# Row gather, cumulative sum and projection: groups of 512 rows instead of whole batches, one cast and one store per group

## The chip, the cores and the metric

The kernel runs on one core of one Trainium2 chip; the other cores are idle. A time is the device time of one execution in microseconds (us). The median of three timed executions is given; a profile is taken in an execution of its own, with every instruction and every DMA packet recorded. Engine names in the profile: PE is TensorE (PEld its weight loads), DVE is VectorE, ACT is ScalarE, POOL is GpSimd, SP is SyncE, which here only issues DMAs.

## The reference

```python
def setup_inputs():
    B, S, N, D = (16, 4096, 2048, 512)
    # x: float32 (B, S, D); indices: int64 (B, N), sorted, distinct; w: float32 (D, D)

def reference(x, indices, w):
    gathered = x[b_idx, indices, :]        # (B, N, D): 2048 of 4096 rows of each batch
    cs = np.cumsum(gathered, axis=1)       # along the 2048 gathered rows
    return np.matmul(cs, w)                # (B, N, D) float32
```

For each of 16 batches, 2048 rows of 512 floats (2 KB each) are fetched by index, summed up cumulatively along the rows, and each sum is multiplied by a 512 x 512 matrix. 67 MB are read and 67 MB written.

## The kernel before

A tile is 128 rows; a batch has NT = 16 tiles, the whole problem 256. The columns are cut into DC = 4 chunks of 128.

- **Indices.** `load_indices(b)` loads one batch's 2048 indices (16 KB, SP's queue), takes the low words as floats on VectorE (L62), transposes them on TensorE (L64) and writes them back as integers, one column per tile (L66). It runs four batches ahead. The weights w (1 MB) are loaded first, on the same queue, and cast to fp16 by VectorE (L51, L52).
- **Gather and cast.** For each tile GpSimd issues an indirect DMA that fetches 128 rows into `g32[:, t, :]` (L79), and ScalarE casts them to fp16 into `g16` (L86). `g32` holds a whole batch (16 tiles, fp32), with two buffers: the first gather of batch b waits until all 16 casts of batch b-2 are done.
- **Cumulative sum.** For each tile four matmuls take the gathered rows as stationary operand and an upper triangle of ones `ut` as moving operand (L93): the result `pa` (PSUM, two buffers) is the sum within the tile, transposed, 128 columns of d by 128 rows for each of four chunks. VectorE adds the last column of the tile before (the carry) and writes fp16 into `csT` (L106; the first tile of a batch is only copied, L103). `csT` too holds a whole batch and has two buffers.
- **Projection.** For each tile four matmuls of 512 columns take `csT` as stationary operand and w as moving operand (L116) and accumulate in `pb` (PSUM, five buffers). Even tiles are copied to `ob` by VectorE (L125), odd ones by ScalarE (L127); then SP stores the 256 KB (L128). `ob` has twelve buffers. Each partition holds one row, so a store is 128 runs of 2 KB.

The program is written out without loops. The framework puts the instructions of each engine in order by a priority, which is the order of writing unless `high_priority` moves it (L101), and by its own estimate of when each is ready; each engine then works in that order. All semaphores are placed by the framework. In the order of writing, a batch's 16 tiles of gathers and casts come first, then 16 of cumulative sums, then 16 of projections.

Of the kernel before, what the change touches and what calls it, by code (L numbers as in the profile page):

```python
# [1 line left out]

# [5 lines left out]

P = 128  # L10
FP32 = mybir.dt.float32
FP16 = mybir.dt.float16
U32 = mybir.dt.uint32


@with_exitstack
def kernel(
    ctx: ExitStack,
    tc: tile.TileContext,
    x: bass.AP,  # L20
    indices: bass.AP,
    w: bass.AP,
    out: bass.AP,
):
    nc = tc.nc

    B, S, D = x.shape
    N = indices.shape[1]
    assert D == 512 and N % P == 0

    NT = N // P
    DC = D // P
    PREF = 3

    x_flat = x.rearrange("b s d -> (b s) d")
    idx_u32 = indices.bitcast(U32)

    const = ctx.enter_context(tc.tile_pool(name="const", bufs=1))
    idxp = ctx.enter_context(tc.tile_pool(name="idxp", bufs=6))
    gp = ctx.enter_context(tc.tile_pool(name="gp", bufs=2))  # L40
    big = ctx.enter_context(tc.tile_pool(name="big", bufs=2))
    outp = ctx.enter_context(tc.tile_pool(name="outp", bufs=12))
    psA = ctx.enter_context(tc.tile_pool(name="psA", bufs=2, space=bass.MemoryType.PSUM))
    psB = ctx.enter_context(tc.tile_pool(name="psB", bufs=5, space=bass.MemoryType.PSUM))

    ut = const.tile([P, P], FP16)
    make_upper_triangular(nc, ut[:], 1.0, diag=True)

    w16 = const.tile([P, DC, D], FP16)
    w32 = const.tile([P, DC, D], FP32)  # L50
    nc.sync.dma_start(out=w32[:], in_=w.rearrange("(c p) d -> p c d", p=P))  # L51
    nc.vector.tensor_copy(out=w16[:], in_=w32[:])  # L52

    id16 = const.tile([16, 16], FP32)
    make_identity(nc, id16[:])
    idxgs = {}

    def load_indices(b):
        idx64 = idxp.tile([16, P], mybir.dt.int64, name="idx64")
        nc.sync.dma_start(out=idx64[:], in_=indices[b].rearrange("(t p) -> t p", p=P))  # L60
        idxf = idxp.tile([16, P], FP32, name="idxf")
        nc.vector.tensor_copy(out=idxf[:], in_=idx64[:].bitcast(U32)[:, 0::2])  # L62
        idx_ps = psB.tile([P, 16], FP32, name="idx_ps", tag="pb")
        nc.tensor.transpose(out=idx_ps[:], in_=idxf[:], identity=id16[:])  # L64
        idxg = idxp.tile([P, NT], U32, name="idxg")
        nc.vector.tensor_copy(out=idxg[:], in_=idx_ps[:])  # L66
        idxgs[b] = idxg

    for bb in range(4):
        load_indices(bb)  # L70

    for b in range(B):
        if b + 4 < B:
            load_indices(b + 4)
        idxg = idxgs.pop(b)
        g32 = gp.tile([P, NT, D], FP32, name="g32")
        g16 = big.tile([P, NT, D], FP16, name="g16")
        for t in range(NT):
            nc.gpsimd.indirect_dma_start(  # L79
                out=g32[:, t, :],  # L80
                out_offset=None,
                in_=x_flat,
                in_offset=bass.IndirectOffsetOnAxis(ap=idxg[:, t : t + 1], axis=0),
                element_offset=b * S * D,
            )
            nc.scalar.copy(out=g16[:, t, :], in_=g32[:, t, :])  # L86

        csT = big.tile([P, DC, N], FP16, name="csT")

        for t in range(NT):  # L90
            pa = psA.tile([P, DC * P], FP32, name="pa")
            for c in range(DC):
                nc.tensor.matmul(  # L93
                    out=pa[:, c * P : (c + 1) * P],
                    lhsT=g16[:, t, c * P : (c + 1) * P],
                    rhs=ut[:],
                    start=(c == 0),
                    stop=(c == DC - 1),
                )
            pa3 = pa[:].rearrange("p (c n) -> p c n", c=DC)  # L100
            with tc.high_priority(offset=200):  # L101
                if t == 0:
                    nc.vector.tensor_copy(out=csT[:, :, 0:P], in_=pa3)  # L103
                else:
                    carry = csT[:, :, t * P - 1 : t * P].broadcast_to([P, DC, P])
                    nc.vector.tensor_tensor(  # L106
                        out=csT[:, :, t * P : (t + 1) * P],
                        in0=pa3,
                        in1=carry,
                        op=mybir.AluOpType.add,  # L110
                    )

        for t in range(NT):
            pb = psB.tile([P, D], FP32, name="pb")
            for c in range(DC):
                nc.tensor.matmul(  # L116
                    out=pb[:],
                    lhsT=csT[:, c, t * P : (t + 1) * P],
                    rhs=w16[:, c, :],
                    start=(c == 0),  # L120
                    stop=(c == DC - 1),
                )
            ob = outp.tile([P, D], FP32, name="ob")
            if t % 2 == 0:
                nc.vector.tensor_copy(out=ob[:], in_=pb[:])  # L125
            else:
                nc.scalar.copy(out=ob[:], in_=pb[:])  # L127
            nc.sync.dma_start(out=out[b, t * P : (t + 1) * P, :], in_=ob[:])  # L128


# [1 line left out]
_INS = ['x', 'indices', 'w']  # L132
_OUTS = [((16, 2048, 512), 'float32')]


# [23 lines left out]
```

## Time and profile before

| | |
|---|---|
| timed executions | 381.35, 381.68, 379.84 us; median 381.35 |
| profiled execution, first to last instruction | 595.4 us; no time of its own beside the span was recorded |
| mean TensorE clock granted in it | 0.776 |
| DMA | 135.96 MB in 58416 packets, 228 GB/s over the span |
| GpSimd gathers (L79) | 256, 949 ns each |
| TensorE projection, cumulative sum (L116, L93) | 1024 of 434 ns, 1024 of 238 ns |
| VectorE carry add (L106), copy (L125) | 240 of 689 ns, 128 of 688 ns |
| ScalarE cast (L86), copy (L127) | 256 of 620 ns, 128 of 586 ns |

The groups of the page read: line, engine, operation, output<-input, shape, count | busy us in all, mean ns of one | idle time of the engine just before them, and who ended it. In the list of waits a row is: who waited <- for whom: us in all, times, longest. In the DMA view a queue's row is: packets, MB, and the time its packets took as a share of 16 DMA engines over the window. q0 is the queue of the gathers, q1 that of SP's loads and stores. The profiled execution is much longer than the timed ones, so a sum made from its rows has to be held against both.

### The profile page before, as it was taken

The numbers are of one execution on the slowest core, as the hardware profiler recorded it, in microseconds if no ns is written. First come the engines' busy times: TensorE is split into PE (matmuls) and PEld (weight loads), VectorE is DVE, ScalarE is ACT, GpSimd is POOL, SyncE is SP. The second block draws the span as 40 slices with busy tenths as digits, with TensorE's granted clock in tenths as the row PEclk, the third lists the DMA queues.
The fourth block names the chain that finished last, engine by engine and source line by source line (L and its number), as shares of the span: only waits on it lengthen the run. The fifth ranks groups of instructions, "written<-read, shape, count | busy, mean of one in ns | idle before, by whom it ended". The sixth has DMA issues, their size and how long they took to land.

```text
span 595.4 us, 6309 instructions
## 1 busy us (share of the span) xinstructions
PE 359.3 (60%) x2064; PEld 177.9 (30%) x2064; DVE 260.1 (44%) x417; ACT 208.7 (35%) x385; POOL 243.7 (41%) x264
## 2 busy tenths in 40 slices
PE   0413653746464791829558284582855838559997
PEld 0201231323232341414224142241422414225553
DVE  2202352425253572516327163361642717339885
ACT  1302353333160453307034070350703507045722
POOL 3772737372717254450714507236072360710000
PEclk9855967566969895868759677596785968869999
DMA  4774969584859678674857748568385684855565
GB/s 141 215 223 143 296 220 295 165 314 162 284 192 307 222 268 293 225 220 177 290 179 243 243 164 288 183 231 263 149 295 187 216 279 189 290 197 211 214 233 227
DMA packets 58416, 135.96 MB, mean 228 GB/s; under 512 B 8464, under 2 KB 8720, under 8 KB 58384
## 3 DMA queue, kind: packets, MB, share of 16 engines
q0 software_dynamic: 20480, 67.13, 37.2%
q1 hardware_dynamic: 37904, 68.44, 30.7%
q8 instruction: 16, 0.26, 0.2%
q14 instruction: 16, 0.13, 0.1%
HBM read 68.42 MB, written 67.11 MB: 228 GB/s over the span
## 4 chain that ended last, share of the span: by engine, by line
PE 49%; another core or an unknown queue 32%; issue 8%; DVE 7%; DMA 2%; POOL 1%; ACT 1%; DVEq 0%; ACTq 0%
PE pb L116 38%; PE pa L93 11%; DVE csT L106 3%; DVE csT L103 2%; DVE ob L125 2%; DMA w<-in_w_dram 1%; POOL g L79 1%; DMA g<-in_x_dram,idxg 1%; ACT ob L127 0%; ACT g L86 0%; DVE w L52 0%; PE idx_ps L64 0%; DVE idxf L62 0%; DVE idxg L66 0%
## 5 line engine op out<-in xcount | busy, mean ns | idle before, releaser
L79 POOL DMA_INDIRECT g<-in_x_dram,idxg x256 | 242.8, 949 | 280.0 <-ACT g L86 198.7
L116 PE MATMUL pb<-w,csT 128*128 128x512 f16 x1024 | 307.6, 434 | 18.9 <-DVE ob L125 13.1
L106 DVE TENSOR_TENSOR csT<-pa,csT 128x512 f16<-128x512 f32 x240 | 165.3, 689 | 148.9 <-remote 91.0
L93 PE MATMUL pa<-ut,g 128*128 128x128 f16 x1024 | 109.0, 238 | 196.1 <-DVE csT L106 91.9
L127 ACT COPY ob<-pb 128x512 f32<-128x512 f32 x128 | 75.1, 586 | 352.6 <-remote 163.8
L93 PEld LDWEIGHTS <-g 128*128 128x128 f16 x1024 | 81.7, 106 | 278.5 <-issue 188.1
L125 DVE COPY ob<-pb 128x512 f32<-128x512 f32 x128 | 87.7, 688 | 164.1 <-remote 87.9
L86 ACT CAST g<-g 128x512 f16<-128x512 f32 x256 | 141.8, 620 | 29.9 <-DMA g<-in_x_dram,idxg 16.5
L116 PEld LDWEIGHTS <-csT 128*128 128x128 f16 x1024 | 103.3, 110 | 111.6 <-issue 61.3
L64 PE MATMUL idx_ps<-id,idxf 16*128 16x16 f32 x16 | 3.4, 252 | 17.1 <-DVE idxf L62 8.3
L103 DVE CAST csT<-pa 128x512 f16<-128x512 f32 x16 | 11.0, 690 | 6.0 <-remote 2.6
L64 PEld LDWEIGHTS idx_ps<-id,idxf 16*128 16x128 f32 x16 | 2.3, 158 | 22.8 <-issue 11.4
L62 DVE CAST idxf<-idx 16x128 f32<-16x128 uint32 x16 | 3.2, 215 | 2.6 <-DMA idx<-in_indices_dram 2.4
L52 DVE CAST w<-w 128x2048 f16<-128x2048 f32 x1 | 1.2, 1227 | 6.8 <-DMA w<-in_w_dram 6.8
L66 DVE CAST idxg<-idx_ps 128x16 uint32<-128x16 f32 x16 | 2.5, 171 | 2.8 <-PE idx_ps L64 2.4
L86 ACT ACT_TABLE_LOAD x1 | 1.3, 1283 | 0.7 <-PEq L143 0.7
masks.py:65 POOL MEMSET ut<- 128x128 f16 x1 | 0.2, 205 | 0.3 <-POOLq L143 0.3
masks.py:66 POOL TENSOR_SCALAR_AFFINE_SELECT ut<-ut 128x128 f16<-128x128 f16 x1 | 0.3, 284 | 0.0
L143 POOL MEMSET const-float32-0.0<- 128x1 f32 x1 | 0.1, 104 | 0.2 <-issue 0.2
masks.py:199 POOL TENSOR_SCALAR_AFFINE_SELECT id<-id 16x16 f32<-16x16 f32 x1 | 0.2, 190 | 0.0
L143 POOL MEMSET const-uint8-127<- 128x1 uint8 x1 | 0.1, 124 | 0.0
L143 POOL MEMSET const-bfloat16-1.0<- 128x1 bf16 x1 | 0.1, 118 | 0.0
(2 smaller groups left out, 0.2 us busy)
## 6 DMA issues: line engine op xcount, KB each, us to landing
out_dram<-ob SPq DMA_DIRECT2D x256, 256.0 KB
g<-in_x_dram,idxg POOLq DMA_INDIRECT x256
w<-in_w_dram SPq DMA_DIRECT2D x1, 1024.0 KB
idx<-in_indices_dram SPq DMA_DIRECT2D x16, 16.0 KB
```

The lines of the kernel that those rows point to most:

```text
L52: nc.vector.tensor_copy(out=w16[:], in_=w32[:])
L62: nc.vector.tensor_copy(out=idxf[:], in_=idx64[:].bitcast(U32)[:, 0::2])
L64: nc.tensor.transpose(out=idx_ps[:], in_=idxf[:], identity=id16[:])
L66: nc.vector.tensor_copy(out=idxg[:], in_=idx_ps[:])
L79: nc.gpsimd.indirect_dma_start(out=g32[:, t, :], out_offset=None, in_=x_flat, in_offset=bass.IndirectOffsetOnAxis(ap=idxg[:, t : t + 1], a ...
L86: nc.scalar.copy(out=g16[:, t, :], in_=g32[:, t, :])
L93: nc.tensor.matmul(out=pa[:, c * P : (c + 1) * P], lhsT=g16[:, t, c * P : (c + 1) * P], rhs=ut[:], start=(c == 0), stop=(c == DC - 1),)
L103: nc.vector.tensor_copy(out=csT[:, :, 0:P], in_=pa3)
L106: nc.vector.tensor_tensor(out=csT[:, :, t * P : (t + 1) * P], in0=pa3, in1=carry, op=mybir.AluOpType.add,)
L116: nc.tensor.matmul(out=pb[:], lhsT=csT[:, c, t * P : (t + 1) * P], rhs=w16[:, c, :], start=(c == 0), stop=(c == DC - 1),)
L125: nc.vector.tensor_copy(out=ob[:], in_=pb[:])
L127: nc.scalar.copy(out=ob[:], in_=pb[:])
```

## The change

The batch as unit is given up. The 256 tiles form 64 groups of R = 4 tiles (512 rows, four groups to a batch), and one loop runs over the groups: the cumulative sum of group g, tile by tile, alternates with the projection of group g-1.

- All indices come in two loads of 128 KB at the start, on SP, and are transposed 128 x 128; w is loaded on ScalarE's queue and cast by ScalarE.
- Gathers have the same form, one per tile, and are written nine groups ahead (`AHEAD`); `g32` holds a group and has nine buffers.
- One ScalarE instruction casts a group's four tiles; `g16` and `csT` hold a group and have four buffers each, `pa` has three.
- The triangle `ut` is reordered, so that row n of a tile goes to column n // 4 of quarter n % 4 of `csT`: after four tiles, the stationary operand j holds the rows 4p + j of the group. The result of projection j then has row 4p + j in partition p, and the four results side by side in `ob` make 8 KB of one partition that are also 8 KB in a row in the output.
- Of a group's four results VectorE copies the first, ScalarE three; one store of 1 MB per group, 128 runs of 8 KB. `ob` holds a group and has five buffers.

```diff
+    R = 4
+    Q = P // R
+    T = B * NT
+    G = T // R
+    GB = NT // R
+    AHEAD = 9
...
-    idxp = ctx.enter_context(tc.tile_pool(name="idxp", bufs=6))
-    gp = ctx.enter_context(tc.tile_pool(name="gp", bufs=2))
-    big = ctx.enter_context(tc.tile_pool(name="big", bufs=2))
-    outp = ctx.enter_context(tc.tile_pool(name="outp", bufs=12))
-    psA = ctx.enter_context(tc.tile_pool(name="psA", bufs=2, space=bass.MemoryType.PSUM))
+    gp = ctx.enter_context(tc.tile_pool(name="gp", bufs=AHEAD))
+    g16p = ctx.enter_context(tc.tile_pool(name="g16p", bufs=4))
+    csp = ctx.enter_context(tc.tile_pool(name="csp", bufs=4))
+    outp = ctx.enter_context(tc.tile_pool(name="outp", bufs=5))
+    psA = ctx.enter_context(tc.tile_pool(name="psA", bufs=3, space=bass.MemoryType.PSUM))
...
+    for k in range(KI):                      # KI = 2
+        nc.sync.dma_start(out=idx64[:, k, :], in_=idx_rows[k * P : (k + 1) * P, :])
+    nc.scalar.dma_start(out=w32[:], in_=w.rearrange("(c p) d -> p c d", p=P))
+    make_identity(nc, ident[:])              # 128 x 128
+    ut = const.tile([P, R, Q], FP16)
+    nc.gpsimd.memset(ut[:], 1.0)
+    nc.gpsimd.affine_select(out=ut[:], in_=ut[:], compare_op=mybir.AluOpType.is_ge, fill=0.0,
+        base=0, pattern=[[1, R], [R, Q]], channel_multiplier=-1)
+    for k in range(KI):
+        nc.vector.tensor_copy(out=idxf[:, k, :], in_=idx64[:, k, :].bitcast(U32)[:, 0::2])
+        nc.tensor.transpose(out=idx_ps[:], in_=idxf[:, k, :], identity=ident[:])
+        nc.vector.tensor_copy(out=idxg[:, k, :], in_=idx_ps[:])
+    nc.scalar.copy(out=w16[:], in_=w32[:])
...
+    def gather(g):
+        g32 = gp.tile([P, R, D], FP32, name="g32")
+        for r in range(R):
+            t = g * R + r
+            nc.gpsimd.indirect_dma_start(out=g32[:, r, :], ...)
+
+    def cumsum_tile(g, r):
+        if r == 0:
+            cst[g] = csp.tile([P, DC, R, P], FP16, name="csT")
+            g16s[g] = g16p.tile([P, R, D], FP16, name="g16")
+            nc.scalar.copy(out=g16s[g][:], in_=gs.pop(g)[:])
+        pa = psA.tile([P, DC, R, Q], FP32, name="pa")
+        for c in range(DC):
+            nc.tensor.matmul(out=pa[:, c], lhsT=g16[:, c * P : (c + 1) * P], rhs=ut[:], ...)
+        dst = csT[:, :, :, r * Q : (r + 1) * Q]
+        ...                                  # first tile of a batch: tensor_copy(dst, pa)
+        nc.vector.tensor_tensor(out=dst, in0=pa[:],
+            in1=last.unsqueeze(2).broadcast_to([P, DC, R, Q]), op=mybir.AluOpType.add)
+
+    def project_tile(g, r):
+        pb = psB.tile([P, D], FP32, name="pb")
+        for c in range(DC):
+            nc.tensor.matmul(out=pb[:], lhsT=csT[:, c, r, :], rhs=w16[:, c, :], ...)
+        if r == 0:
+            nc.vector.tensor_copy(out=obs[g][:, r, :], in_=pb[:])
+        else:
+            nc.scalar.copy(out=obs[g][:, r, :], in_=pb[:])
+        if r == R - 1:
+            b, h = divmod(g, GB)
+            dst = out[b, h * R * P : (h + 1) * R * P, :].rearrange("(p j) d -> p j d", j=R)
+            nc.sync.dma_start(out=dst, in_=obs.pop(g)[:])
+
+    for g in range(AHEAD):
+        gather(g)
+    for g in range(G + 1):
+        if g + AHEAD < G:
+            gather(g + AHEAD)
+        for r in range(R):
+            if g < G:
+                cumsum_tile(g, r)
+            if g > 0:
+                project_tile(g - 1, r)
```

The `high_priority` block around the carry add is gone, and so is the per-batch `load_indices`.

More of the change, by code (lines that the diff above doesn't have):

```diff
@@ L6 @@
 from concourse import bass_utils, mybir
-from concourse.masks import make_upper_triangular, make_identity
+from concourse.masks import make_identity
 from concourse._compat import with_exitstack
@@ L41 @@
-    big = ctx.enter_context(tc.tile_pool(name="big", bufs=2))
-    outp = ctx.enter_context(tc.tile_pool(name="outp", bufs=12))
-    psA = ctx.enter_context(tc.tile_pool(name="psA", bufs=2, space=bass.MemoryType.PSUM))
-    psB = ctx.enter_context(tc.tile_pool(name="psB", bufs=5, space=bass.MemoryType.PSUM))
-    ut = const.tile([P, P], FP16)
-    make_upper_triangular(nc, ut[:], 1.0, diag=True)
-    w16 = const.tile([P, DC, D], FP16)
-    w32 = const.tile([P, DC, D], FP32)
-    nc.sync.dma_start(out=w32[:], in_=w.rearrange("(c p) d -> p c d", p=P))
@@ L52 @@
[L52 to L78, printed above, removed]
+    gp = ctx.enter_context(tc.tile_pool(name="gp", bufs=AHEAD))
+    g16p = ctx.enter_context(tc.tile_pool(name="g16p", bufs=4))
+    csp = ctx.enter_context(tc.tile_pool(name="csp", bufs=4))
+    outp = ctx.enter_context(tc.tile_pool(name="outp", bufs=5))
@@ new lines @@
+    ident = const.tile([P, P], FP32)
+    make_identity(nc, ident[:])
+    ut = const.tile([P, R, Q], FP16)
+    nc.gpsimd.memset(ut[:], 1.0)
+    nc.gpsimd.affine_select(
+        out=ut[:],
+        in_=ut[:],
+        compare_op=mybir.AluOpType.is_ge,
+        fill=0.0,
+        base=0,
+        pattern=[[1, R], [R, Q]],
+        channel_multiplier=-1,
+    )
+    idxf = const.tile([P, KI, P], FP32)
+    idxg = const.tile([P, KI, P], U32)
+    for k in range(KI):
+        nc.vector.tensor_copy(out=idxf[:, k, :], in_=idx64[:, k, :].bitcast(U32)[:, 0::2])
+        idx_ps = psB.tile([P, P], FP32, name="idx_ps", tag="pb")
+        nc.tensor.transpose(out=idx_ps[:], in_=idxf[:, k, :], identity=ident[:])
+        nc.vector.tensor_copy(out=idxg[:, k, :], in_=idx_ps[:])
@@ L79 @@
+    w16 = const.tile([P, DC, D], FP16)
+    nc.scalar.copy(out=w16[:], in_=w32[:])
+    gs = {}
+    cst = {}
+    g16s = {}
+    def gather(g):
+        g32 = gp.tile([P, R, D], FP32, name="g32")
+        gs[g] = g32
+        for r in range(R):
+            t = g * R + r
             nc.gpsimd.indirect_dma_start(
-                out=g32[:, t, :],
+                out=g32[:, r, :],
                 out_offset=None,
                 in_=x_flat,
-                in_offset=bass.IndirectOffsetOnAxis(ap=idxg[:, t : t + 1], axis=0),
@@ L84 @@
-                element_offset=b * S * D,
-            )
[L86 to L128, printed above, removed]
+                in_offset=bass.IndirectOffsetOnAxis(ap=idxg[:, t // P, t % P : t % P + 1], axis=0),
@@ new lines, in gather @@
+                element_offset=(t // NT) * S * D,
+            )
+    def cumsum_tile(g, r):
[3 more added lines that the diff above has]
+            nc.scalar.copy(out=g16s[g][:], in_=gs.pop(g)[:])
+        csT = cst[g]
+        g16 = g16s[g][:, r]
+        pa = psA.tile([P, DC, R, Q], FP32, name="pa")
+        for c in range(DC):
+            nc.tensor.matmul(
+                out=pa[:, c],
+                lhsT=g16[:, c * P : (c + 1) * P],
+                rhs=ut[:],
+                start=(c == 0),
+                stop=(c == DC - 1),
+            )
+        dst = csT[:, :, :, r * Q : (r + 1) * Q]
+        if g % GB == 0 and r == 0:
+            nc.vector.tensor_copy(out=dst, in_=pa[:])
+            return
+        if r == 0:
+            last = cst[g - 1][:, :, R - 1, P - 1 : P]
+        else:
+            last = csT[:, :, R - 1, r * Q - 1 : r * Q]
+        nc.vector.tensor_tensor(
+            out=dst,
+            in0=pa[:],
+            in1=last.unsqueeze(2).broadcast_to([P, DC, R, Q]),
+            op=mybir.AluOpType.add,
+        )
@@ new lines @@
+    obs = {}
+    def project_tile(g, r):
+        if r == 0:
+            obs[g] = outp.tile([P, R, D], FP32, name="ob")
+        csT = cst[g]
+        pb = psB.tile([P, D], FP32, name="pb")
+        for c in range(DC):
+            nc.tensor.matmul(
+                out=pb[:],
+                lhsT=csT[:, c, r, :],
+                rhs=w16[:, c, :],
+                start=(c == 0),
+                stop=(c == DC - 1),
+            )
+        if r == 0:
+            nc.vector.tensor_copy(out=obs[g][:, r, :], in_=pb[:])
+        else:
+            nc.scalar.copy(out=obs[g][:, r, :], in_=pb[:])
[3 more added lines that the diff above has]
+            nc.sync.dma_start(out=dst, in_=obs.pop(g)[:])
```

13 lines of the change are left out of this document (9 added, 4 removed).

## The prediction

> **What bounds the kernel now.** I read the page first (engines, queues, chain, groups), then the waits, then the timeline of the start and of the end, then the DMA queues in single windows.
>
> ```profile
> span 595.4 us, 6309 instructions
> PE 359.3 (60%) x2064; PEld 177.9 (30%) x2064; DVE 260.1 (44%) x417; ACT 208.7 (35%) x385; POOL 243.7 (41%) x264
> ...
> DMA packets 58416, 135.96 MB, mean 228 GB/s; under 512 B 8464, under 2 KB 8720, under 8 KB 58384
> ...
> PE 49%; another core or an unknown queue 32%; issue 8%; DVE 7%; DMA 2%; POOL 1%; ACT 1%; DVEq 0%; ACTq 0%
> ...
> L79 POOL DMA_INDIRECT g<-in_x_dram,idxg x256 | 242.8, 949 | 280.0 <-ACT g L86 198.7
> L116 PE MATMUL pb<-w,csT 128*128 128x512 f16 x1024 | 307.6, 434 | 18.9 <-DVE ob L125 13.1
> L106 DVE TENSOR_TENSOR csT<-pa,csT 128x512 f16<-128x512 f32 x240 | 165.3, 689 | 148.9 <-remote 91.0
> L93 PE MATMUL pa<-ut,g 128*128 128x128 f16 x1024 | 109.0, 238 | 196.1 <-DVE csT L106 91.9
> L127 ACT COPY ob<-pb 128x512 f32<-128x512 f32 x128 | 75.1, 586 | 352.6 <-remote 163.8
> ...
> L125 DVE COPY ob<-pb 128x512 f32<-128x512 f32 x128 | 87.7, 688 | 164.1 <-remote 87.9
> L86 ACT CAST g<-g 128x512 f16<-128x512 f32 x256 | 141.8, 620 | 29.9 <-DMA g<-in_x_dram,idxg 16.5
> ```
>
> The profiled execution is not the timed one: 595.4 us against a median of 381.35. No engine is over 60% busy, and 32% of the chain (191 us) is time whose releaser the trace does not know. So I look for what 381 us can hold, and that starts with GpSimd.
>
> ```profile
> POOL g L79 <- ACT g L86: 198.7, 14, 18.1
> ...
> POOL g L79 <- issue: 73.1, 239, 0.6
> ```
>
> ```profile
> L79 POOL DMA_INDIRECT g<-in_x_dram,idxg x256: 943/949/1102, 9.0 to 523.4; - x128
> ```
>
> ```profile
> L128 SPq DMA_DIRECT2D out_dram<-ob x256: 332/332/1004, 28.3 to 592.0; - x128
> ```
>
> The four rows are two of the list of waits, one of the gather's line, one of the store's. The gathers' train runs from 9.0 to 523.4 us: 242.8 busy, 73.1 of the 0.30 us gap between two gathers, 198.7 in 14 waits for ScalarE's casts to free one of the two 16-tile g32 buffers. The pitch is (242.8+73.1)/256 = 1.234 us, and 1.25 within a batch. From the last gather to the end are 72 us. Without the 14 waits the profiled execution would be 595.4-198.7 = 396.7. The timed 381.35 leave, after a head of 9.0 and a train of 315.9, 56.4 us for the tail and all waits of GpSimd together. So in timed runs the train hardly waits, and the time is head + train + tail. What the tail is, the end of the trace shows, where no gather disturbs:
>
> ```profile
> 554.20:572.90 18.70, 18.14 (x132) 9.77 (x130) 15.67 (x25) 9.08 (x18) 0.00 (x0) 1.00 0.62 235
> ```
>
> One batch of 16 tiles there takes 18.70 us (columns: length, then busy time of TensorE, weight loads, VectorE, ScalarE, GpSimd, granted clock, DMA share, GB/s): TensorE is busy 18.14 at full clock, 1.17 us a tile. When the last gather is issued, up to two batches are still to be projected, because a batch's cumsum of 16 tiles stands ahead of its projection: 2 x 18.7 = 37.4 us, and some of the 56.4 are then waits.
>
> The DMA engines are the second candidate.
>
> ```profile
> DMA packets 1177, 3.04 MB, mean 380 GB/s; under 512 B 188, under 2 KB 188, under 8 KB 1177
> ...
> q0 software_dynamic: 621, 2.03, 69.5%
> q1 hardware_dynamic: 556, 1.01, 32.8%
> ```
>
> ```profile
> q1 hardware_dynamic: 5904, 10.75, 60.1%
> ```
>
> The first fence is the DMA view of 221 to 229 us, the stretch with both queues fullest; the second that of 545 to 592, stores alone. Stores: 10.75 MB in 0.601 x 47 = 28.2 us, 381 GB/s while busy, 0.69 us for 256 KB. Gathers beside stores: 2.03 MB in 0.695 x 8 = 5.56 us, 365 GB/s, 0.72 us. Both at once moved 380 GB/s: 0.524 MB a tile, 1.38 us. That is more than the gather's pitch of 1.25, so the two limits lie within 10% of each other. The timed runs bound it too: (381.35-9.0-37.4)/256 = 1.31 us a tile with a two-batch tail, 1.38 with a one-batch tail.
>
> **The change part by part.**
>
> *Start.* Before, 1 MB of w is loaded ahead of the indices, and w's cast stands ahead of the first index cast:
>
> ```profile
> 0.75 5.99 DMA w<-in_w_dram
> 6.76 1.23 DVE w L52
> 9.03 1.10 POOL g L79
> 15.47 2.99 DMA g<-in_x_dram,idxg
> ```
>
> ```profile
> 7.90 0.75 DVE L62 CAST idxf<-idx 16x128 f32<-16x128 uint32 x5
> ```
>
> ```profile
> masks.py:65 POOL MEMSET ut<- 128x128 f16 x1 | 0.2, 205 | 0.3 <-POOLq L143 0.3
> masks.py:66 POOL TENSOR_SCALAR_AFFINE_SELECT ut<-ut 128x128 f16<-128x128 f16 x1 | 0.3, 284 | 0.0
> ```
>
> These are pieces of the chain of waits, one row of the timeline and two groups of the page. After, the indices come as two 128 KB loads first on SP, w on ScalarE's queue beside them. If they share the rings evenly they land as w did, near 6.0, if not near 2.5; with the 1.13 us from the index cast to the first gather (7.90 to 9.03 before) the train starts between 3.6 and 7.1. I take 5.5, a gain of 3.5. The larger masks on GpSimd, two fills and selects of 128 x 128, take 2 x (0.2+0.3) = 1 us and end before the indices land, even at 2.5; without that cover they would cost the 1 us. w's cast moves to ScalarE, which has no group to cast before 5.5 + 4 x 1.25 + 3 = 13.5 us. Sixteen small index casts, transposes and copies inside the loop become two ahead of it; none was on the path.
>
> *Gathers.* 256 of the same form, same pitch: floor 256 x 1.25 = 320. Their buffer is freed by a group's cast instead of the whole batch's 16: 36 tiles ahead (45 us of train) instead of two lumps of 16. The 198.7 us of waits go; late next is the landing of packets. The new wait, of gather g+9 for cast g, holds up only later gathers.
>
> *Casts.* ScalarE casts 2048 columns at once.
>
> ```profile
> 314.10 2.18 ACT L86 CAST g<-g 128x512 f16<-128x512 f32 x4
> 6.76 1.23 DVE L52 CAST w<-w 128x2048 f16<-128x2048 f32 x1 [6.76 <-DMA w<-in_w_dram]
> ```
>
> Four back to back take 2.18 us, which bounds the new one from above; VectorE's 1.23 for the same shape bounds it from below. I take 2.1, nearer to its own engine: 64 x 2.1 = 134 instead of 141.8.
>
> *Cumsum.* The same matmuls (1024 of 128 columns) and the same 256 VectorE instructions of 128 x 512. Their writes now go in runs of 32 columns instead of 128. No row shows that; I take 689 ns as before. Twice that is the other end: VectorE would need 1.55 us a tile and decide (below).
>
> *Projection and copies.* The same 1024 matmuls. VectorE keeps 64 copies, ScalarE gets 192: VectorE 176+44 = 220 us, ScalarE 134+192 x 0.586 = 247 us. Both stay under the train's 320 and cost nothing beside it; without that cover ScalarE would have 247 to give. TensorE at 1.17 us a tile needs 299 us, also under it, if its clock stays up.
>
> *Stores.* 64 of 1 MB in place of 256 of 256 KB: same bytes, SP has 192 issues of 0.33 us less, off the path. 8 KB runs mean a quarter of the 32,768 store packets. No row has such packets. The ends for 256 KB: a small loss, down to the gathers' 365 GB/s (0.72 us), or a gain at which gather and store fit into GpSimd's pitch (1.25-0.72 = 0.53), beyond which nothing more is won. Nothing in the rows moves faster than 381 GB/s while busy, so I take a small gain, 0.65, and 1.38 becomes 1.34. A store now waits for four copies instead of one; behind it on SP stand only later stores, and an ob buffer is wanted again five groups (26 us) later.
>
> *Train.* Pace between 1.25 (GpSimd) and 1.34 (rings full); 1.29, the middle: 256 x 1.29 = 330.
>
> *Tail.* The last group alone: landing 3.0 (row above), cast 2.1, cumsum of 4 tiles beside the projection of the group before 4 x 1.17 = 4.7, projection 4 x 4 x 0.216 = 3.5, last copy 0.6, then the 1 MB store. A 256 KB store ended 3.4 us after its issue (592.0 to 595.4), 0.69 of it transfer: 2.7 + 1 MB at 380 GB/s, 2.8 = 5.5.
>
> ```profile
> 586.57 4.76 PE pb L116 x22
> ```
>
> This row gives the 0.216 (4.76/22). Sum of the tail 19.4, against at least 37.
>
> *Sum.* 5.5 + 330 + 19.4 = 355 us. Against the timed median that is -26 (head -3.5, tail -18 or more, pace the rest), against the profiled 595.4 it says nothing, since its idle is not in the timed runs.
>
> **The rivals.**
>
> *GpSimd alone decides.* If the rings keep up: 5.5 + 320 + 19.4 = 345, or a little less. For it: gathers never stretch, 943 to 1102 ns.
>
> *The bytes decide.* 135.96 MB in 381.35 us are 356 GB/s already. If that is what the memory gives two mixed streams, the change moves the same bytes and only the head goes: 378. Against it: the 380 GB/s above, over 8 us only; for it:
>
> ```profile
> 248.00:252.00 4.00, 3.09 (x4) 1.00 1.01 322
> ```
>
> In this stretch in the middle of the trace (length, GpSimd's busy time, granted clock, DMA share, GB/s) rings that are full move 322 GB/s.
> The Trainium skill's page "DMA: Bandwidth & Descriptors", section "Where 436 GB/s comes from", says that for transfers between HBM and SBUF a core's share of about 358 GB/s binds; by it 136 MB need 380 us, and nothing would be gained. The trace's 380 GB/s speaks against it for a core alone on the chip.
>
> *The cast is exposed (slower).* ScalarE works in order. If the cast of group g+1 stands behind the last copy of group g-1, TensorE can't start the cumsum of g+1 until it is done: 4.7 of TensorE + 0.6 + 2.1 in series = 7.4 us a group in place of 5.2, 64 x 7.4 + 25 = 499; half exposed, near 425. It decides once a group takes over 5.6 us ((381-25)/64), so from 0.9 us exposed. TensorE's clock would add to it, as it falls where TensorE idles:
>
> ```profile
> 300.00:302.00 2.00, 0.00 (x0) 0.00 (x0) 0.00 (x0) 0.00 (x0) 1.03 (x2) 0.50 0.88 273
> ```
>
> In this stretch the four engines ahead of GpSimd did nothing, and the clock granted was 0.50. VectorE at twice 689 ns gives 64 x 4 x 1.55 + 25 = 422, on the same side. Against both: four g16 and four csT buffers let the cast run ahead, and before, casts and copies were interleaved freely.
>
> **How the numbers follow.** Forecast (345 to 366) 0.66; GpSimd alone (336 to 345) 0.08; bytes (366 to 384) 0.12, half of it within 0.5% of now; slower (390 to 500) 0.14. A measurement of this kernel can tell about 0.5%, since its three times span 1.84 us. Faster 0.80, same 0.06, slower 0.14. Range 340 to 378: it leaves out the slower cases and the edges.
>
> **What would show it.** Right: gathers x256 at about 949 ns whose waits for casts are a few us in all; 64 casts near 2.1 us; 64 stores, about 8,192 packets of them; last gather to end near 20 us; first gather before 7 us. Wrong: TensorE waiting on ScalarE's cast once a group; a cumsum add over 0.9 us; rings full at under 350 GB/s; a first gather later than 9 us.

## The result and the profile after

After: 366.76, 367.82, 369.49 and 369.94 us, median 368.65. Before, timed beside it: median 380.62. Ratio 0.967, interval [0.962, 0.972]: 12 us faster, where 26 were forecast.

The profile that the prediction reads (595.4 us) was not taken beside these times. In some sessions the kernel before takes 560 to 594 us (medians), and the change brings 13% there (560.43 to 488.78; experiment 7); from here on the two kernels are compared in sessions where the one before takes 381.

The page of the kernel after (the execution took 369.94 us, of which 368.2 are the span):

```profile
span 368.2 us, 5777 instructions
...
PE 298.0 (81%) x2050; PEld 163.8 (44%) x2050; DVE 216.5 (59%) x324; ACT 219.5 (60%) x258; POOL 243.2 (66%) x264
...
DMA  4678989999999999999999999999999999999675
...
DMA packets 30541, 135.92 MB, mean 369 GB/s; under 512 B 5168, under 2 KB 5424, under 8 KB 22320
...
L140 PE MATMUL pb<-w,csT 128*128 128x512 f16 x1024 | 269.3, 387 | 45.2 <-ACT ob L150 43.5
L93 POOL DMA_INDIRECT g<-in_x_dram,idxg x256 | 242.1, 946 | 90.7 <-issue 59.7
L125 DVE TENSOR_TENSOR csT<-pa,csT 128x512 f16<-128x512 f32 x240 | 165.4, 689 | 59.3 <-PE pa L110 51.8
L105 ACT CAST g<-g 128x2048 f16<-128x2048 f32 x64 | 121.5, 1899 | 127.8 <-DMA g<-in_x_dram,idxg 103.9
...
L150 ACT COPY ob<-pb 128x512 f32<-128x512 f32 x192 | 100.8, 589 | 10.3 <-PE pb L140 9.5
```

The groups are where they were forecast: the gather costs the same, the cast 1.90 us for four tiles, the add 689 ns although it now writes runs of 32 columns. The DMA engines' row (40 slices of the span, tenths) is full from slice 7 to 37 and not before or behind; that is where to look.

A profile of the kernel before from a session of the same kind (379.86 us, span 378.1) gives a comparison that the first one could not give. Each fence holds three rows of one kernel: the gathers' train (first and last start), the projections that start behind the last gather, and the middle of the span in one window (length; busy time of TensorE, weight loads, VectorE, ScalarE, GpSimd; granted clock, DMA share, GB/s). Before, then after:

```profile
L79 POOL DMA_INDIRECT g<-in_x_dram,idxg x256: 942/946/1101, 8.8 to 327.7; - x128
...
L116 PE MATMUL pb<-w,csT x163: 379/379/380, 327.5 to 373.6; 128*128 128x512 f16 x163
...
96.00:312.00 216.00, 192.17 (x1303) 101.55 (x1301) 160.04 (x254) 132.68 (x243) 163.30 (x174) 0.97 1.04 403
```

```profile
L93 POOL DMA_INDIRECT g<-in_x_dram,idxg x256: 940/946/1098, 7.7 to 333.6; - x128
...
L140 PE MATMUL pb<-w,csT x100: 376/379/390, 333.7 to 362.1; 128*128 128x512 f16 x100
...
96.00:312.00 216.00, 188.75 (x1335) 104.46 (x1333) 139.93 (x208) 140.56 (x168) 158.07 (x168) 0.99 1.01 406
```

| us | before | after | difference | forecast for after |
|---|---|---|---|---|
| head, to the first gather | 8.8 | 7.7 | -1.1 | 5.5 |
| train, first to last gather | 318.9 | 325.9 | +7.0 | 330 |
| tail, last gather to the end | 50.4 | 34.6 | -15.8 | 19.4 |
| span | 378.1 | 368.2 | -9.9 | 355 |

Four matmuls are a tile. When the last gather is issued, 163/4 = 41 tiles of projection are left before and 100/4 = 25 after. In the middle both kernels have full rings (DMA share 1.04 and 1.01), and these move 403 and 406 GB/s. The gain comes from the tail: work that no longer stands behind the last gather. More of it stood there still than was forecast.

The list of waits and the end of ScalarE's timeline say why 25 tiles are left:

```profile
PE pb L140 <- ACT ob L150: 43.5, 50, 3.9
...
ACT g L105 <- DMA g<-in_x_dram,idxg: 103.9, 49, 6.7
```

```profile
337.97 1.90 ACT L105 CAST g<-g 128x2048 f16<-128x2048 f32 x1 [1.65 <-DMA g<-in_x_dram,idxg]
339.78 1.55 ACT L150 COPY ob<-pb 128x512 f32<-128x512 f32 x3
343.56 1.90 ACT L105 CAST g<-g 128x2048 f16<-128x2048 f32 x1 [2.23 <-DMA g<-in_x_dram,idxg]
345.37 2.04 ACT L150 COPY ob<-pb 128x512 f32<-128x512 f32 x4
...
362.56 0.59 ACT L150 COPY ob<-pb 128x512 f32<-128x512 f32 x1 [0.28 <-PE pb L140]
```

ScalarE works in its order: one cast, three copies, one cast, three copies. The three copies behind the cast of group g are the last one of group g-5 and two of group g-4. While ScalarE stands at a cast and waits for its gather (103.9 us in all), the copies behind it wait too, the `pb` buffers stay full, and TensorE waits 43.5 us for them. TensorE never catches up; behind the last cast stand 16 copies (4 and then 12), 5.3 groups. From 346.0 us on the chain of waits is TensorE alone:

```profile
346.00 1.02 PE pb L140 x4
347.02 0.22 PE pa L110 x4
...
358.11 4.43 PE pb L140 x20
362.54 0.02 issue
362.56 0.59 ACT ob L150
```

So the tail of 34.6 us has two parts. The last gather starts at 333.6 and its cast at 343.56: 9.9 us. From there to the end are 24.6 us. In these TensorE works off 16 tiles of projection (64 matmuls from 346.00 on; the forecast counted 8, the last group and the one before it), in turn with 11 tiles of cumulative sum, of which 7 belong to groups ahead of the last one.

### The profile page after: what moved, and what is told of

It reads as the page before. It is cut to its first block, busy times and chain, and to the rows that moved or that the text cites. A ratio compares the mean times of both kernels' runs of the same rounds, so it can differ in the third digit from the quotient of the medians.

```text
span 368.2 us, 5777 instructions
## 1 busy us (share of the span) xinstructions
PE 298.0 (81%) x2050; PEld 163.8 (44%) x2050; DVE 216.5 (59%) x324; ACT 219.5 (60%) x258; POOL 243.2 (66%) x264
## 2 busy tenths in 40 slices
DMA packets 30541, 135.92 MB, mean 369 GB/s; under 512 B 5168, under 2 KB 5424, under 8 KB 22320
## 5 line engine op out<-in xcount | busy, mean ns | idle before, releaser
L140 PE MATMUL pb<-w,csT 128*128 128x512 f16 x1024 | 269.3, 387 | 45.2 <-ACT ob L150 43.5
L105 ACT CAST g<-g 128x2048 f16<-128x2048 f32 x64 | 121.5, 1899 | 127.8 <-DMA g<-in_x_dram,idxg 103.9
L140 PEld LDWEIGHTS <-csT 128*128 128x128 f16 x1024 | 93.4, 99 | 116.8 <-issue 57.3
L110 PEld LDWEIGHTS <-g 128*128 128x128 f16 x1024 | 80.6, 100 | 74.3 <-ACT g L105 13.1
L110 PE MATMUL pa<-ut,g 128*128 128x128 f16 x1024 | 101.3, 224 | 12.5 <-ACT g L105 12.5
L150 ACT COPY ob<-pb 128x512 f32<-128x512 f32 x192 | 100.8, 589 | 10.3 <-PE pb L140 9.5
L148 DVE COPY ob<-pb 128x512 f32<-128x512 f32 x64 | 44.3, 692 | 60.2 <-PE pb L140 60.2
L78 PE MATMUL idx_ps<-ident,idxf 128*128 128x128 f32 x2 | 0.9, 462 | 6.8 <-DVE idxf L76 6.8
L82 ACT CAST w<-w 128x2048 f16<-128x2048 f32 x1 | 1.9, 1898 | 4.3 <-DMA w<-in_w_dram 4.3
```

The costliest lines, as they stand in the source:

```text
L78: nc.tensor.transpose(out=idx_ps[:], in_=idxf[:, k, :], identity=ident[:])
L82: nc.scalar.copy(out=w16[:], in_=w32[:])
L105: nc.scalar.copy(out=g16s[g][:], in_=gs.pop(g)[:])
L110: nc.tensor.matmul(out=pa[:, c], lhsT=g16[:, c * P : (c + 1) * P], rhs=ut[:], start=(c == 0), stop=(c == DC - 1),)
L140: nc.tensor.matmul(out=pb[:], lhsT=csT[:, c, r, :], rhs=w16[:, c, :], start=(c == 0), stop=(c == DC - 1),)
L148: nc.vector.tensor_copy(out=obs[g][:, r, :], in_=pb[:])
```

## The experiments

Theory L: the lag of the cumulative sum and the projection behind the casts, put into ScalarE's order by the four buffers of the fp16 group, makes the tail longer than forecast. Its rivals: the bytes alone decide, the stores' run length matters, or the head does.

**1. Two buffers for the fp16 group.** ScalarE's order then has 10 copies (3.3 groups) behind the last cast instead of 16. (The expectations count a group less throughout: 7, 13 and 19 for two, four and six buffers.)

```diff
-    g16p = ctx.enter_context(tc.tile_pool(name="g16p", bufs=4))
+    g16p = ctx.enter_context(tc.tile_pool(name="g16p", bufs=2))
```

> The changed kernel with two buffers for the cast rows. Where the kernel before takes 380 us and the changed one 368: theory L (the tail is the groups left behind the last cast) about 360, last gather to end about 26 us instead of 34.6; rival B (rings decide) 366 or more; rival C (cast exposed) over 375. Where the kernel before takes 560 or more: the same as the changed kernel within 1%, as before.

Measured: 359.83 us, ratio to before 0.943 [0.939, 0.947], 8.8 us less than the kernel after.

```profile
L93 POOL DMA_INDIRECT g<-in_x_dram,idxg x256: 940/946/1101, 7.5 to 332.2; - x128
...
L140 PE MATMUL pb<-w,csT x68: 376/379/389, 331.9 to 350.8; 128*128 128x512 f16 x68
...
96.00:312.00 216.00, 197.21 (x1347) 101.38 (x1345) 141.83 (x211) 141.28 (x169) 159.40 (x170) 1.00 1.02 410
```

```profile
PE pa L110 <- ACT g L105: 35.4, 48, 9.6
```

The last landing and the last projections in the chain of waits, and the last cast on ScalarE's timeline:

```profile
332.17 8.62 DMA g<-in_x_dram,idxg
...
346.74 4.43 PE pb L140 x20
```

```profile
340.89 1.90 ACT L105 CAST g<-g 128x2048 f16<-128x2048 f32 x1 [1.33 <-DMA g<-in_x_dram,idxg]
```

Seventeen tiles are left behind the last gather, and the tail is 358.2 - 332.2 = 26.0, as theory L expected. Behind the last cast 8 tiles of projection are left, and the last group's cumulative sum follows its cast directly (TensorE's first of its four tiles starts at 342.84, the cast ends at 342.79): this is the order that the prediction had assumed. TensorE now waits for the casts, 48 times, which the prediction had named as a bad sign; here it is a good one, since it means that TensorE has caught up with the gathers.

**2. Six buffers**, the same line with 6: 22 copies, 7.3 groups, behind the last cast.

> The changed kernel with six instead of four buffers for the fp16 group. In ScalarE's order 19 copies (6.3 groups) then follow the last cast, instead of 13 (4.3 groups); with two buffers it was 7 (2.3 groups). The span from the last cast to the end was 17.3 us with two buffers and 24.6 with four, so 3.65 us for each group that the projection runs late. Theory L (the projection's lag behind the casts sets the tail): about 32 us behind the last cast, 7 us more than the changed kernel, a ratio to the kernel before near 0.986 (376 us where that takes 381). Rival S (two buffers were faster for another reason, and the lag costs nothing beyond four because csT has four buffers that hold the cumsum back anyway): 0.967, no later than the changed kernel.

Measured: 374.95 us, 0.983 [0.980, 0.986], 6.3 us more than the kernel after by the medians. The last landing in the chain of waits, the last cast on ScalarE's timeline, and the waits:

```profile
330.65 9.39 DMA g<-in_x_dram,idxg
```

```profile
340.14 1.90 ACT L105 CAST g<-g 128x2048 f16<-128x2048 f32 x1 [1.63 <-DMA g<-in_x_dram,idxg]
```

```profile
PE pb L140 <- ACT ob L150: 49.4, 53, 5.3
```

From the last cast to the end: 17.3 us with two buffers (10 copies), 24.6 with four (16), 33.4 with six (22); 3.7 and 4.4 us for each further group, near the 4.35 us that TensorE needs for a group's cumsum and projection. Theory L holds in both directions, and rival S falls. The other part of the tail, from the last gather's start to its cast, differs by 1.2 us at most: 8.7, 9.9 and 9.5.

**3. w's load behind the index loads.** In the kernel after, w shares the rings with the indices.

```diff
-    nc.scalar.dma_start(out=w32[:], in_=w.rearrange("(c p) d -> p c d", p=P))
+    nc.sync.dma_start(out=w32[:], in_=w.rearrange("(c p) d -> p c d", p=P))
```

> The changed kernel with w's load behind the index loads on SP's queue. Where the changed one takes 368 us: first gather near 5 us instead of 7.72; theory L 365 to 366, rival B (rings decide) over 367. Where the kernel before takes 560 or more: no difference to be told from the spread of a few us.

Measured: 365.0 us, 0.957 [0.953, 0.960], 3.6 us less than the kernel after. The start of the timeline, after and with this edit:

```profile
4.01 0.23 DVE L76 CAST idxf<-idx 128x128 f32<-128x128 uint32 x1 [4.01 <-DMA idx<-in_indices_dram]
...
7.01 0.23 DVE L76 CAST idxf<-idx 128x128 f32<-128x128 uint32 x1 [2.77 <-DMA idx<-in_indices_dram]
7.15 0.28 DVE L79 CAST idxg<-idx_ps 128x128 uint32<-128x128 f32 x1
...
7.72 1.10 POOL L93 DMA_INDIRECT g<-in_x_dram,idxg  x1 [5.98 <-DVE idxg L79]
```

```profile
3.01 0.23 DVE L76 CAST idxf<-idx 128x128 f32<-128x128 uint32 x1 [3.01 <-DMA idx<-in_indices_dram]
...
3.48 0.23 DVE L76 CAST idxf<-idx 128x128 f32<-128x128 uint32 x1 [0.24 <-DMA idx<-in_indices_dram]
...
4.45 1.10 POOL L93 DMA_INDIRECT g<-in_x_dram,idxg  x1 [2.70 <-DVE idxg L79]
```

After, the second index load lands 3 us behind the first, and VectorE's order has its cast (7.01) ahead of the write-back that the first gather needs (7.15). With w behind, both have landed by 3.5. The head is 3.3 us shorter, the span 3.0 (365.2), as theory L expected.

**4. 2 KB runs.** The store of a group as four DMAs of one tile each, as long a run as before the change.

```diff
-            nc.sync.dma_start(out=dst, in_=obs.pop(g)[:])
+            ob = obs.pop(g)
+            for j in range(R):
+                nc.sync.dma_start(out=dst[:, j, :], in_=ob[:, j, :])
```

> The changed kernel with four stores of 256 KB of 2 KB runs per group. Where the changed one takes 368 us with full rings: 376 to 380 if the packets set the pace (309 ns for 8 KB against 4 x 84), 368 to 370 if GpSimd does. Where the kernel before takes 560 or more: 0.5 to 1.5% slower than the changed kernel, as before.

Measured: 371.04 us, 0.970 [0.965, 0.976], 2.4 us more than the kernel after, with overlapping intervals. It lies 5 us below the 376 to 380 of packets that set the pace, and 1 us above the other forecast.

```profile
L93 POOL DMA_INDIRECT g<-in_x_dram,idxg x256: 942/946/1098, 7.8 to 326.7; - x128
...
L140 PE MATMUL pb<-w,csT x137: 379/379/390, 326.5 to 364.3; 128*128 128x512 f16 x137
...
96.00:312.00 216.00, 185.46 (x1314) 101.52 (x1313) 136.54 (x205) 141.76 (x169) 163.30 (x174) 1.00 1.04 405
```

```profile
DVE ob L148 <- DMA out_dram<-ob: 40.0, 29, 2.4
...
ACT ob L150 <- DMA out_dram<-ob: 30.8, 17, 2.5
```

Two rows of the pages' DMA issues, with the median from issue to landing of a gather, with 2 KB runs and in the kernel after:

```profile
g<-in_x_dram,idxg POOLq DMA_INDIRECT x256, 6.3
```

```profile
g<-in_x_dram,idxg POOLq DMA_INDIRECT x256, 8.3
```

The rings move 405 GB/s against 406: the run length does not buy bandwidth that shows. It changes who waits. With 2 KB runs the gathers go at GpSimd's own pitch (a train of 318.9 us, as before the change), and the copies wait 70.8 us for stores to free `ob`, so 34 tiles are left at the end. With 8 KB runs the stores keep up, and the gathers take 7 us longer, and land in 8.3 us instead of 6.3.

**5. Both edits (1 and 3).**

> Two buffers for the fp16 group and w's load behind the index loads on SP's queue. Alone they gave 0.943 and 0.9565 of the kernel before, against 0.967 of the changed kernel: 8.8 and 3.6 us. If the two edits act at the two ends of the span (the first gather near 4.4 us, the tail of 26 us), they add: 356 us where the kernel before takes 381, a ratio near 0.934. If the rings set the pace of the train (134 MB at some 415 GB/s is 323 us), an earlier first gather only fills the rings earlier and half of the 3.6 us is lost: 0.939.

Measured: 357.1 us, 0.938 [0.933, 0.944], the best version: 11.5 us below the kernel after, as much again as the change brought. First gather 4.6, last 329.2, end 355.3. Against experiment 1 the span is 2.9 us shorter, the head 2.9; so by the two profiles the head's gain comes through whole. The ratio, 0.938, lies nearer to the other case (0.939), but its interval holds both, so the times do not decide it.

**6. Both edits and 4 KB runs**: the store as two DMAs of two tiles each.

> As the run with both edits, with each group's store in two DMAs of two tiles each, so that a run in HBM is 4 KB long, as long as a gather's. Theory Q (the two rings are served packet by packet, so the longer packet has the greater share): a gather landed 8.3 us after its issue beside 8 KB stores and 6.2 us beside 2 KB stores, in the page's medians, and the train from the first to the last gather took 326 and 319 us; beside 4 KB stores a gather lands in about 7 us, the train takes 319 to 322 us, and the stores fall behind a little, so the tail is 1 to 4 us longer: the time within 3 us of the run with both edits. Rival C (the cost of a packet decides, not its share): gathers land as beside 8 KB stores, near 8.3 us, the train stays near 325 us, and the time is up by half of the 2.4 us that 2 KB runs cost.

Measured: 358.21 us, 0.940 [0.936, 0.944]; 1.1 us over experiment 5, and the same within the intervals.

```profile
L93 POOL DMA_INDIRECT g<-in_x_dram,idxg x256: 940/947/1099, 4.4 to 331.2; - x128
...
g<-in_x_dram,idxg POOLq DMA_INDIRECT x256, 9.2
```

Theory Q falls for this size: the gathers do not land sooner beside 4 KB runs (9.2 us against 8.8 in experiment 5), and the train is 326.8 us, not 319 to 322. The train is what rival C forecast (near 325); that a packet's cost is the reason is not shown. What sets the 2 KB case apart stays open. The Trainium skill, page "DMA: Bandwidth & Descriptors", section "Queues, rings and completion order", says that an engine changes between queues packet by packet; section "SWDGE vs HWDGE vs iDMA" says, of GpSimd's path, that a packet is preferably at most 4096 B. If SP's stores were cut likewise, a run of 8 KB would go as two packets, and the 4 and 8 KB cases would be alike, as they are; why the 2 KB case differs, this does not say. No run here shows packets in that sense: the trace has one record of 309 ns (median) for 8 KB, 159 for 4 and 84 for 2.

**7. Sessions in which everything is longer.** Eight runs fell in two sessions where the kernel before takes 594 and 560 us by the median. In the first, the kernel before once more:

> The kernel before, unchanged, profiled once more. The first profile of it spans 595.4 us, the timed runs 381. Theory L (the predicted pace was right, and the tail of the changed kernel is what was mis-sized): a profile near 380 us shows a train of gathers of about 256 x 1.28 = 328 us after a start at 9 us, and so a tail of about 40 us after the last gather. Rival B (the bytes decide): full rings at under 370 GB/s from the first store to the last, and a tail no longer than 25 us. If the span is near 595 us again, the recording itself slows this kernel, and nothing more is learned of its timed runs.

566.83 us against a median of 594.13 there. That the recording itself slows the kernel does not follow: in the other sessions it was recorded at 379.86 us. The edits of 1, 3 and 4:

> The changed kernel with two buffers for the cast rows (g16) instead of four. In ScalarE's order the last cast is then followed by the copies of about 2.3 groups instead of 4.3. Theory L (the tail is the groups that the order leaves to project after the last cast, 4.35 us of TensorE each): last gather to end falls from 34.6 to about 26 us, the time by 8 to 9 us, to about 360. Rival B (the rings decide; their packets fill 348 of 368 us): stores come earlier, the gathers slow down by as much, and the time falls by under 3 us. Rival C (the cast is exposed with fewer buffers): TensorE waits for casts once a group, and the time rises above 375.

> The changed kernel with the load of w on SP's queue behind the two index loads, instead of beside them on ScalarE's queue. All theories: the indices land near 3 us, the first gather is issued near 5 us instead of 7.72. Theory L: every gather and the end come that much earlier, the time falls by 2 to 3 us, to about 366. Rival B: w's 1 MB is then moved beside the first gathers, and the time falls by under 1 us.

> The changed kernel with four stores of 256 KB per group, each of 128 runs of 2 KB, instead of one store of 1 MB with 8 KB runs; all else as it was. Theory L with full rings (a packet of 8 KB takes 309 ns, four of 2 KB took 4 x 84 = 336 in the first profile of the kernel before): the pace rises from 1.28 to about 1.32 us a tile, the time by 8 to 12 us, to about 378. Rival (GpSimd's pitch of 1.25 us decides the pace): no change within 2 us.

487.76, 488.44 and 496.95 us, ratios to before 0.823, 0.823 and 0.842 [0.834, 0.851]. The kernel after is not among them, so these three say nothing on theory L; the second session has it beside them:

> The kernel before, unchanged, profiled beside the others. Where it takes about 380 us: theory L expects a train of gathers of about 328 us (pace 1.28) after a start at 9 us, hardly any waits of GpSimd for casts, and about 40 us from the last gather to the end. Rival B (the bytes decide): rings full at under 370 GB/s to within 25 us of the end.

> The changed kernel, unchanged, as the reference for the runs beside it: where the kernel before takes 380 us, about 368; last gather to end about 35 us, first gather at 7.7 us, rings at 400 to 417 GB/s in the middle. Where the kernel before takes 590 us: near 490, since the three variants of it took 484 to 497 there.

> The changed kernel with two buffers for the cast rows instead of four; ScalarE's order then leaves the copies of about 2.3 groups behind the last cast instead of 4.3. Theory L: the tail falls from 34.6 to about 26 us and the time by 8 to 9 us against the changed kernel beside it. Rival B (rings decide): the gathers slow down by as much as the tail gains, under 3 us. Rival C: the cast is exposed, slower.

> The changed kernel with four stores of 256 KB of 2 KB runs per group. If full rings set the pace (packet of 8 KB 309 ns, four of 2 KB 336 ns): 8 to 12 us slower than the changed kernel beside it. If GpSimd's pitch of 1.25 us sets it: no change within 2 us.

Before 557.83 (median there 560.43); after 488.78, two buffers 485.86, 2 KB runs 491.1. The edits are within 1% of the kernel after there. Theory L's 8 to 9 us did not come, only 2.9: the tail is 58.5 us with two buffers and 61.3 with four. The greater part of the additional time is not the tail: in the kernel after the span is 116 us longer than in the result's profile, and the train alone 89 (415.2 against 325.9). The waits of VectorE in the kernel after:

```profile
DVE csT L125 <- PE pa L110: 77.9, 97, 3.3
DVE csT L125 <- remote: 74.8, 27, 21.0
```

The second row is waits for a signal whose sender the trace does not know. Measured to the start of a tile's add from the end of its last cumsum matmul, or from where VectorE comes free if that is later, one in ten adds starts over 2.0 us late there and none in the result's profile (its 99th percentile is 0.11 us). The kernel before once more, in a session like that of the result (the table above uses it):

> The kernel before, profiled beside the others, since the two profiles taken so far beside its timed runs show it at 557 to 567 us and not at 380. Where it takes about 380: theory L expects a train of gathers of about 328 us (pace 1.28 us a tile) after a start at 9 us, and about 40 us from the last gather to the end. Rival B (the bytes decide): full rings at under 370 GB/s to within 25 us of the end. Where it takes 560 or more: TensorE's signals to VectorE late by microseconds, as in the profiles so far.

Why signals come late in some sessions was not settled; no run here takes a cause away. The chip itself is not shown to be the cause: the results give the chip's number as 10 and 1 in the long sessions, and as 0 and again 1 in the short ones.

## Why the prediction was half right

- *Direction and range* were right (368.65 lies in 340 to 378), and so was where to look: head, train, tail. But 368.65 lies above the forecast's 345 to 366 (0.66), in the band that was given to the bytes (0.12), and the gain is 12 us where 26 were forecast.
- *The step that failed is "Tail. The last group alone"*: 19.4 us forecast, 34.6 taken. These 15.2 us, with the head's 2.2 more and the train's 4.1 less, are the 13.3 between 354.9 (its 355) and the span of 368.2. Two of its parts were wrong, the overlap and the landing.
  - *The overlap*, 8 of the 15 us: the last group was to follow its cast directly, and that with 8 tiles of projection behind the cast, 16.4 us to the end; 16 tiles stood there, and it took 24.6. The projection does keep about one group behind the cumsum, as the loop is written (five tiles, 4.43 us, stand behind the last cumsum), but the cumsum itself does not follow the cast: ScalarE's order has the casts run ahead. The prediction held four `g16` buffers for protection ("let the cast run ahead"); the experiments with two, four and six show that they are the price: tails of 26.0, 34.6 and 42.9 us.
  - *The landing*, 7 of the 15 us: 3.0 us was the row of an early gather (15.47 us), before any store was under way; among stores the last one takes 9.9 from its start to its cast, 0.95 of it on GpSimd. No experiment changes that part on purpose, and with two buffers it is what keeps the tail at 26.0: 8.7 and then 17.3, where 3.0 and 16.4 were forecast.
- *The tail before* was taken as part of 56.4 us "for the tail and all waits of GpSimd together". It was 50.4 us of tail, 41 tiles, and no waits to speak of. The prediction's sum gave the tail's gain as "-18 or more", from a tail of at least 37; it is -15.8, with both ends some 13 to 15 us longer than sized, so that the gain came near the figure by luck.
- *Head*: 5.5 forecast, 7.7 taken, 0.6 us outside the bounds of 3.6 to 7.1. The loads did share the rings, the first gather waited for the second index load too, and the term took a value too near the good end; the landing near 2.5 had no row, and experiment 3 shows 3.0 and a first gather at 4.4.
- *Train*: 330 forecast, 325.9 taken, 1.27 us a tile, between the 1.25 of GpSimd and the 1.34 that the prediction gave full rings. That it came so near is in part luck: full rings moved 406 GB/s, 1.29 us a tile, where the prediction had 380 and 1.38 and took off a gain of the 8 KB runs that did not come. ("Nothing in the rows moves faster than 381 GB/s" holds for the rows it shows; in the same profile a slice of 0.6 us of w's load moved 410.) Its sum has "pace the rest", a gain of some 4 us, but the train lost 7 us against before: there GpSimd was never held up (318.9 us), and the copies waited instead, 75 us, for stores to free `ob`:

```profile
ACT ob L127 <- DMA out_dram<-ob: 42.6, 34, 2.6
DVE ob L125 <- DMA out_dram<-ob: 32.7, 24, 2.2
```

- *Casts*: 2.1 forecast, 1.90 measured. The row had bounded it; the Trainium skill's page "ScalarE: Activation LUTs", section "What ACT_TABLE_LOAD costs", gives 186 ns + 0.833 ns a column for an instruction with immediate scale and bias; worked out from it, an estimate of 1.89 us for 2048 columns, and the trace agrees with 1.899.
- *8 KB runs*: the 64 stores are there, and 30541 - 22320 = 8221 packets of 8 KB or more. They were sized at 0.65 against 0.69 us for 256 KB, 3% of the 1.38 us a tile. The full rings moved 406 against 405 GB/s, and the whole is worth 2.4 us by the medians, with overlapping intervals.
- *The rival "the bytes decide"* (378) had the mechanism half right. The two kernels' full rings carry the same 403 and 406 GB/s, so the 134.2 MB of gathers and stores take 333 and 331 us. But of the spans 45 and 38 us lie beside that, and these can be cut: to 355.3 - 134.2 MB/410 GB/s = 28 us in experiment 5. The 358 GB/s of the Trainium skill, which the prediction weighed, do not bind here: 403 to 410 were moved. The Trainium skill's "HBM Reference", section "Specifications (TRN2)", has the case: a core streaming alone gets about 425 GB/s, two of a pair about 358 each; the 403 to 410 GB/s here lie nearer to the first, and no run loads the pair.
- *The rival "GpSimd alone"* (345): its train of 320 us came with 2 KB runs, 318.9, and the time was 371.04, since 34 tiles then stood behind the last gather.
- *The slower rivals*: TensorE did not wait once a group for a cast (12.5 us in two waits), and the add did not slow down (689 ns). With two buffers it did wait at 48 casts, and the kernel was faster.

## What to carry to other kernels

When an engine that works in order serves two stages, look up how many instructions of the later stage stand behind its last instruction of the earlier one: that backlog is added to the tail, and a deeper buffer between the stages can lengthen it. Take the time from the last load's issue to its landing from a stretch with full rings, not from one of the first loads. Count, in the trace, the work left when the last load is issued; with full rings in the middle, what the experiments here could cut was that count and the head. A wait of the last stage for fresh data was a good sign here, a wait for its own output buffers a bad one.

## What the runs showed of the hardware

- Gathers and stores together move 403 to 410 GB/s over 216 us, with stores in runs of 2, 4 or 8 KB (84, 159 and 309 ns a record). Shorter runs shifted the wait from gathers to stores, and left the rate.
- VectorE's add of 128 x 512 takes 689 ns whether it writes runs of 128 or of 32 columns.
- Gathers landed later beside stores: 3.0 us for an early one of the prediction's profile, before the first store; 6.3 in the median beside stores of 2 KB runs and 8.3 beside 8 KB runs.
- The same program takes 369 us in one session and 489 in another, and the kernel before 381 and 560 to 594. In the longer ones VectorE and ScalarE wait for signals whose sender the trace does not know; TensorE is busy 68% of the kernel after instead of 81%, and its mean granted clock is lower (0.837 against 0.978). An edit's value belongs to the session: two buffers bring 2.4% in one, 0.6% in the other.
